# A two-layer diffusion trunk on one core: an output projection of eight full blocks, weight low parts by a fused operation, and mixing roots by ScalarE's ln and exp

## The chip, the core and the metric

The kernel runs on one core of a Trainium2 chip. The core has TensorE (PE; its weight loads stand in a row of their own, PEld), VectorE (DVE), ScalarE (ACT), GpSimd (POOL) and SyncE (SP), which here issues the DMAs. Each engine works through its own queue in order; semaphores tie them together. The metric is the device time of one execution in microseconds (us), the median of several runs.

## The reference, cut to what matters

A trunk of two layers works on 128 context tokens and 256 latent tokens together (T = 384). Each layer is a SwiGLU half, a token mixing, and a second SwiGLU half, each behind an RMSNorm with shift, scale and gate from a conditioning vector. The mixing projects the tokens once, runs three head groups (A: grouped attention; B: gated linear attention; C: differential attention) and projects their joined outputs back:

```
q, k of A and C:  x * rsqrt(mean(x*x) + EPS) * g          per head
out_a = softmax attention,              width 6 x 64 = 384
out_b = rms_norm(o_b, g_gla) * silu(b_r), width 4 x 64 = 256
out_c = rms_norm(out_c, g_c_out) * (1 - lam_init), width 4 x 96 = 384
out   = concatenate([out_a, out_b, out_c]) @ w_out        (1024 x 1024)
x     = x + gate * out
```

## The kernel before, in words

Activations lie transposed, 128 features on the partitions and 384 tokens along the row, in eight tiles `x[k]`. Each matmul with weights is done in three pieces (`mm3`): weights and activations are split into a high part that TensorE takes in its fp32r form and a low part that holds the rest, and high x high, high x low and low x high are summed in PSUM. `load_split` loads a weight tile (`wraw`, five buffers), ScalarE rounds the high part (`whi`, three buffers), VectorE subtracts to get the low part (`wlo`, three buffers). In the feed-forward halves VectorE also sums products for the modulation vectors (L254), and GpSimd subtracts the low parts of activations (`alo`, L477).

A mixing (`mixing`) is cut into named stages, and `ORDER` gives the order in which each layer's stages are written. `br`, `bq`, `bk`, `bv`, `wa`, `wv`, `wq` and `wk` are projections, `lg`, `de`, `st`, `L0` to `L6` and `go` belong to group B, `c0` to `c3` are the four heads of group C, `n0` and `n1` their norms (two heads each), `s0` and `s1` the splits into high and low parts, `p0` to `p2` and `o0` to `o2` the attention of group A. Tile, the layer that issues the program, keeps the data dependences and orders each engine's instructions by its own plan, so stages overlap. `lg` asks for ScalarE's table set with natural log and exp.

The inverse roots come from `newton`, all on VectorE: a first value by integer arithmetic on the bits, then three steps of three operations, 13 operations in all on 12 or 24 columns. A mixing has seven: one in `make_rstd`, one in `qk_norm` for each of `wa`, `wq`, `wk`, and one in `rsq_bcast` for `n0`, `n1` and `go` (which spreads the root over a row by transposes).

The projection reads nine blocks of 128 rows in the order of `KORD`: three of A, two of B, and four of C, one per head, of 96 rows, with the weights' last 32 rows of such a block at zero and not used. For each of eight output tiles it takes two loads, of five and four blocks:

```
for k0, k1 in ((0, 5), (5, 9)):
    w = load_split(I["wo"][l, m][:, k0 * P:k1 * P], (k1 - k0) * P)
    for k in range(k0, k1):
        n, hi, lo = mo[k]
        mm3(ps, w[0][:n, c:c + P], w[1][:n, c:c + P], hi, lo, k == 0, k == 8)
end_tile(l, 1, m, ps, acc, nxt, None)
```

Of the kernel before, what the change touches and what calls it, by code (L numbers as in the profile page):

```python
# [27 lines left out]
EPS = 1e-6  # L28
# [18 lines left out]
TW = T + 2  # L47
# [7 lines left out]
NPT = 3  # L55
# [5 lines left out]
NRM = (0, 1)  # L61
HV = (1, 1, 1, 1, 1, 1, 1, 1)
ORDER = (
    ("ha br bq hb bk wq bv lg rq de wk st L0 rk L1 cx wa wv L2 c0 L3 c1 L4 c2 ra L5 L6 n0 s0 c3 n1 p0 ax "
     "s1 go o0 p1 p2 o1 o2").split(),
    ("br ha hb bq bk bv lg L0 wq rq wk de L1 st rk L2 wa cx wv L3 c0 ra L4 c1 c2 L5 c3 n0 L6 p0 ax "
     "go o0 p1 s0 p2 o1 n1 s1 o2").split(),
)
KORD = (
    ("c0 c1 c2 c3 b0 b1 a0 a1 a2").split(),  # L70
    ("a0 b0 b1 c0 c1 a1 c2 c3 a2").split(),
)


# [7 lines left out]
def _build(ctx, tc, nc, I, O):  # L82
# [213 lines left out]

    def load_split(src, cols=WCOL):
        raw = wp.tile([P, WCOL], F32, tag="wraw", bufs=NRAW, name="wraw")
        di = nc.sync.dma_start(out=raw[:, :cols] if len(src.shape) == 2 else
                               raw[:, :cols].rearrange("p (j c) -> p j c", j=src.shape[1]), in_=src)  # L300
        hi = wp.tile([P, WCOL], F32R, tag="whi", bufs=3, name="whi")
        lo = wp.tile([P, WCOL], F32R, tag="wlo", bufs=3, name="wlo")
        S.activation(out=hi[:, :cols], in_=raw[:, :cols], func=AF.Copy)  # L303
        vi = V.tensor_tensor(out=lo[:, :cols], in0=raw[:, :cols], in1=hi[:, :cols].bitcast(F32), op=ALU.subtract)  # L304
        return hi, lo, vi, di

    def mm3(ps, lh, ll, rh, rl, start, stop):
# [4 lines left out]
    def newton(pool, ss, n, scale, parts, tag):  # L312

        m = pool.tile([P, n], F32, tag=tag + "m", name="nm")[:parts]
        V.tensor_scalar(out=m, in0=ss, scalar1=scale, scalar2=EPS, op0=ALU.mult, op1=ALU.add)
        s = pool.tile([P, n], I32, tag=tag + "s", name="ns")[:parts]
        V.tensor_scalar(out=s, in0=m.bitcast(I32), scalar1=1, scalar2=None, op0=ALU.logical_shift_right)
        y = pool.tile([P, n], F32, tag=tag + "y", bufs=2, name="ny")[:parts]
        V.tensor_scalar(out=y.bitcast(I32), in0=s, scalar1=-1.0, scalar2=float(0x5f3759df), op0=ALU.mult, op1=ALU.add)
        mh = pool.tile([P, n], F32, tag=tag + "h", name="nh")[:parts]  # L320
        V.tensor_scalar(out=mh, in0=m, scalar1=-0.5, scalar2=None, op0=ALU.mult)
        for _ in range(3):
            a = pool.tile([P, n], F32, tag=tag + "a", name="na")[:parts]
            V.tensor_tensor(out=a, in0=y, in1=y, op=ALU.mult)
            V.tensor_tensor(out=a, in0=a, in1=mh, op=ALU.mult)
            y2 = pool.tile([P, n], F32, tag=tag + "y", bufs=2, name="ny")[:parts]
            V.scalar_tensor_tensor(out=y2, in0=a, scalar=1.5, in1=y, op0=ALU.add, op1=ALU.mult)
            y = y2
        return y

    def rsq_bcast(pool, srcs, cols, scale, parts, tag, t, r):
# [5 lines left out]
        y = newton(pool, t.rearrange("p n (a b) -> p (n a) b", b=32)[:, :, 0], n * nb, scale, parts, tag)  # L337
# [223 lines left out]
    def mixing(l, us, acc, nxt):  # L561
        turn["own"] = {"mm": ("both",), "ax": ("ada",)}
        r_ = make_rstd(acc)
        with tc.tile_pool(name=f"mix{l}", bufs=1) as mp:
            def mt(shape, tag, bufs=1, dt=F32):
                return mp.tile(shape, dt, tag=tag, bufs=bufs, name=tag)
# [9 lines left out]
            s0 = mt([P, 2, 64], "s0")  # L576
# [79 lines left out]
            def qk_norm(pss, parts, n, d):  # L656

                w = n * d
                ss = mt([P, 3, 8], "ss", 2)
                xs = []  # L660
                for t, ps in enumerate(pss):
                    xg = t512()
                    for c, hn, gd, g in parts:
                        V.tensor_tensor(out=xg[:, c:c + hn * gd].rearrange("p (h d) -> p h d", h=hn),
                                        in0=ps[:, c:c + hn * gd].rearrange("p (h d) -> p h d", h=hn),
                                        in1=g[:, None, :].to_broadcast([P, hn, gd]), op=ALU.mult)
                    sq = t512(w)
# [3 lines left out]
                y = newton(mp, ss.rearrange("p a b -> p (a b)"), 24, 1.0 / d, P, "q")  # L671
# [78 lines left out]
            def a_out(i, pts):  # L750
                po = (mmps if PMM[6 + i] else axps)()[:, :T]
                for k in range(4):
                    for g in range(2):
                        r = slice(64 * g, 64 * g + 64)
                        if k == 0:
                            PE.matmul(po[r, 0:P], lhsT=av[:, 0, r], rhs=ptx[:, g, i, :], start=True, stop=True)
                        else:
                            PE.matmul(po[r, P:T], lhsT=av[:, k, r], rhs=pts[g][:, k - 1, :],  # L758
                                      start=(k == 1), stop=(k == 3))
                hi = hp.tile([P, TW], F32R, tag="h", name="ohi")[:, :T]  # L760
                S.activation(out=hi, in_=po, func=AF.Copy)
# [48 lines left out]
            cp = {}  # L810

            def c_first(j):
                cp[j] = mt([P, 2, T], "oc", 2)[:96], mt([P, 2, T], "pt", NPT)[:96], []
                c_next(j, 0)

            def c_next(j, i):
                oc, osq, pss = cp[j]
                c_head(2 * j + i, oc[:, i, :], osq[:, i, :], pss)

            def c_norm(j):  # L820
                oc, osq, pss = cp[j]
                r = rsq_bcast(mp, pss, T, 1.0 / 96, 96, "c", osq, osq)
                V.scalar_tensor_tensor(out=oc, in0=oc, scalar=gco[:96], in1=r, op0=ALU.mult, op1=ALU.mult)

            def c_split(j):
                oc = cp[j][0]
                for i in range(2):
                    hi = hp.tile([P, TW], F32R, tag="h", name="chi")[:96, :T]
                    S.activation(out=hi, in_=oc[:, i, :], func=AF.Copy)
                    lo = hp.tile([P, TW], F32R, tag="h", name="clo")[:96, :T]  # L830
                    V.tensor_tensor(out=lo, in0=oc[:, i, :], in1=hi.bitcast(F32), op=ALU.subtract)
                    moc.append((96, hi, lo))
# [112 lines left out]
            def gla_out():  # L945
# [31 lines left out]
                for i in range(2):  # L977
                    hi = hp.tile([P, TW], F32R, tag="h", name="bhi")[:, :T]
                    lo = hp.tile([P, TW], F32R, tag="h", name="blo")[:, :T]
                    S.activation(out=hi, in_=ot[:, i, :], func=AF.Copy)  # L980
                    V.tensor_tensor(out=lo, in0=ot[:, i, :], in1=hi.bitcast(F32), op=ALU.subtract)
                    mob.append((P, hi, lo))

            sv = {}

# [81 lines left out]


            turn["own"] = {"mm": ("both",), "ax": ()}
            mo = [{"a": moa, "b": mob, "c": moc}[n[0]][int(n[1])] for n in KORD[l]]  # L1070
            acc = new_acc()
            us = []
            for m in range(KT):
                ps = mmps()[:, :T]
                for k0, k1 in ((0, 5), (5, 9)):
                    w = load_split(I["wo"][l, m][:, k0 * P:k1 * P], (k1 - k0) * P)
                    for k in range(k0, k1):
                        c = (k - k0) * P
                        n, hi, lo = mo[k]
                        mm3(ps, w[0][:n, c:c + P], w[1][:n, c:c + P], hi, lo, k == 0, k == 8)  # L1080
# [138 lines left out]
```

## Time and profile before

| | |
|---|---|
| median of three timed runs | 1589.09 us (1588.32 to 1589.89) |
| the profiled execution's own time | 1599.75 us |
| its span, first to last instruction | 1597.9 us |
| PE busy | 1563.3 us, 9370 matmuls |
| DVE busy | 1229.3 us, 2294 instructions |
| ACT busy | 738.8 us, 1444 instructions |
| POOL busy | 196.2 us, 239 instructions |
| mean granted TensorE clock | 0.980 |

Busy times are sums over stages that differ; matmul ends are modelled, so a busy PE is not yet PE at its peak. The first layer's mixing lies at about 314 to 533 us of the span, the second's at about 1096 to 1315 us; all else is feed-forward. The granted clock is a share of 2.4 GHz; it is 1.0 or, at 1.2 GHz, 0.5.

### The profile page before, as it was taken

The numbers are of one execution on the slowest core, as the hardware profiler recorded it, in microseconds if no ns is written. First come the engines' busy times: TensorE is split into PE (matmuls) and PEld (weight loads), VectorE is DVE, ScalarE is ACT, GpSimd is POOL, SyncE is SP. The second block draws the span as 40 slices with busy tenths as digits, with TensorE's granted clock in tenths as the row PEclk, the third lists the DMA queues.
The fourth block names the chain that finished last, engine by engine and source line by source line (L and its number), as shares of the span: only waits on it lengthen the run. The fifth ranks groups of instructions, "written<-read, shape, count | busy, mean of one in ns | idle before, by whom it ended". The sixth has DMA issues, their size and how long they took to land.

```text
span 1597.9 us, 25055 instructions
## 1 busy us (share of the span) xinstructions
PE 1563.3 (98%) x9370; PEld 1464.0 (92%) x9370; DVE 1229.3 (77%) x2294; ACT 738.8 (46%) x1444; POOL 196.2 (12%) x239
## 2 busy tenths in 40 slices
PE   7999999999999999999999999999999999999999
PEld 5999999997558999999999999999875699999999
DVE  4799999888766888898968889667787767666532
ACT  4544433365466544443344444335546754444321
POOL 1211130030000211111001111102000011111100
PEclk9999999999789999999999999999898999999999
DMA  9677778542104566666666666543321064443441
GB/s 330 231 229 229 226 225 261 165 122 83 45 1 140 168 197 202 201 192 207 204 213 197 210 197 195 174 144 96 113 77 39 1 230 144 143 137 130 120 143 57
DMA packets 83230, 256.38 MB, mean 160 GB/s; under 512 B 10978, under 2 KB 19746, under 8 KB 82722
## 3 DMA queue, kind: packets, MB, share of 16 engines
q1 hardware_dynamic: 83108, 254.78, 50.3%
q8 instruction: 74, 1.21, 0.3%
q14 instruction: 48, 0.39, 0.1%
HBM read 251.99 MB, written 2.75 MB: 159 GB/s over the span
## 4 chain that ended last, share of the span: by engine, by line
PE 90%; DVE 6%; ACT 2%; issue 1%; DMA 1%; POOL 1%; SPq 0%; DVEq 0%; ACTq 0%; POOLq 0%
PE mm L308 20%; PE mm L310 20%; PE mm L309 20%; PE both L308 7%; PE both L309 7%; PE both L310 7%; PE mm L789 1%; DVE wlo L304 1%; PE ax L803 1%; PE ax L901 1%; PE ax L721 1%; DVE junk L254 1%; PE ax L807 0%; DVE ht L397 0%; PE ax L758 0%
## 5 line engine op out<-in xcount | busy, mean ns | idle before, releaser
L303 ACT ACTIVATE whi<-wraw 128x1024 fp32r<-128x1024 f32 (+4 forms) x358 | 348.4, 975 | 461.2 <-PE mm L309 259.1
L304 DVE TENSOR_TENSOR wlo<-wraw,whi 128x1024 fp32r<-128x1024 f32 (+4 forms) x358 | 451.8, 1264 | 131.0 <-ACT whi L303 129.0
L310 PE MATMUL mm<-h,wlo 128*128 128x386 f32 x1096 | 373.3, 341 | 2.5 <-DVE wlo L304 2.5
L308 PE MATMUL mm<-h,whi 128*128 128x386 f32 x1096 | 372.8, 341 | 2.6 <-POOL h L367 1.4
L309 PE MATMUL mm<-h,whi 128*128 128x386 f32 x1096 | 372.5, 340 | 0.0
L254 DVE SCALAR_TENSOR_TENSOR junk<-araw,cb 128x1024 f32<-128x1024 f32 x256 | 312.3, 1220 | 0.8
L310 PEld LDWEIGHTS mm<-h,wlo 128*128 128x128 f32 x1096 | 208.0, 190 | 4.2 <-DVE wlo L304 3.5
L308 PEld LDWEIGHTS mm<-h,whi 128*128 128x128 f32 x1096 | 207.6, 190 | 4.6 <-ACT whi L303 1.7
L309 PEld LDWEIGHTS mm<-h,whi 128*128 128x128 f32 x1096 | 207.6, 189 | 1.6 <-issue 0.7
L477 POOL TENSOR_TENSOR alo<-s,ahi 128x384 fp32r<-128x384 f32 x88 | 115.5, 1314 | 641.5 <-ACT ahi L475 614.9
L309 PE MATMUL mm<-alo,whi 128*128 128x384 f32 x528 | 177.9, 337 | 0.0
L310 PE MATMUL mm<-ahi,wlo 128*128 128x384 f32 x528 | 177.9, 337 | 0.0
L308 PE MATMUL mm<-ahi,whi 128*128 128x384 f32 x528 | 177.9, 337 | 0.0
L308 PE MATMUL both<-h,whi 128*128 128x386 f32 x360 | 122.5, 340 | 0.0
L309 PE MATMUL both<-h,whi 128*128 128x386 f32 x360 | 122.1, 339 | 0.0
L310 PE MATMUL both<-h,wlo 128*128 128x386 f32 x360 | 122.0, 339 | 0.0
L475 ACT ACTIVATE ahi<-s 128x384 fp32r<-128x384 f32 x88 | 46.3, 526 | 129.4 <-DVE s L472 129.3
L309 PEld LDWEIGHTS mm<-alo,whi 128*128 128x128 f32 x528 | 99.2, 188 | 0.0
L310 PEld LDWEIGHTS mm<-ahi,wlo 128*128 128x128 f32 x528 | 99.2, 188 | 0.0
L308 PEld LDWEIGHTS mm<-ahi,whi 128*128 128x128 f32 x528 | 99.2, 188 | 0.0
L469 DVE TENSOR_TENSOR u<-mm,rstd 128x384 f32<-128x384 f32 x66 | 36.6, 554 | 60.8 <-PE mm L310 60.8
L467 ACT ACTIVATE s<-s,bc 128x128 f32<-128x128 f32 (+1 forms) x176 | 70.7, 449 | 8.0 <-ACT bc L418 0.7
(365 smaller groups left out, 2446.7 us busy)
## 6 DMA issues: line engine op xcount, KB each, us to landing
wraw<-in_wgu SPq DMA_DIRECT2D x170, 512.0 KB, 4.2
araw<-in_w_adat SPq DMA_DIRECT2D x128, 512.0 KB, 4.0
wraw<-in_wd SPq DMA_DIRECT2D x64, 512.0 KB, 4.2
wraw<-in_wd SPq DMA_DIRECT2D x32, 384.0 KB, 3.5
araw<-in_w SPq DMA_DIRECT2D x16, 512.0 KB, 5.6
wraw<-in_wo SPq DMA_DIRECT2D x16, 320.0 KB, 3.0
wraw<-in_wit SPq DMA_DIRECT2D x8, 512.0 KB, 3.4
wraw<-in_wa SPq DMA_DIRECT2D x8, 512.0 KB, 3.6
```

What stands on the lines that cost most here:

```text
L254: V.scalar_tensor_tensor(out=junk, in0=w, scalar=1.0, in1=self.cb[:, c, :], op0=ALU.mult, op1=ALU.mult, accum_out=self.acc[:, f, c:c + 1])
L303: S.activation(out=hi[:, :cols], in_=raw[:, :cols], func=AF.Copy)
L304: vi = V.tensor_tensor(out=lo[:, :cols], in0=raw[:, :cols], in1=hi[:, :cols].bitcast(F32), op=ALU.subtract)
L308: PE.matmul(ps, lhsT=lh, rhs=rh, start=start, stop=False)
L309: PE.matmul(ps, lhsT=lh, rhs=rl, start=False, stop=False)
L310: return PE.matmul(ps, lhsT=ll, rhs=rh, start=False, stop=stop)
L467: S.activation(out=s[:, a:b], in_=s[:, a:b], func=AF.Silu, bias=bg[:, c:c + 1])
L469: vi = V.tensor_tensor(out=u, in0=pu[:, :T], in1=r, op=ALU.mult)
L475: S.activation(out=hi, in_=s, func=AF.Copy)
L477: G.tensor_tensor(out=lo, in0=s, in1=hi.bitcast(F32), op=ALU.subtract)
L721: pi = PE.transpose(ps[:, i * P:(i + 1) * P], p[:, i, :], ident)
L789: PE.matmul(pp[m], lhsT=qtc[r, h, (t + 1) * P:(t + 2) * P], rhs=ktc[r, h, 0:T], start=True, stop=True)
```

## The change

The four C heads are packed into three blocks of 128 rows: heads 0 to 2 keep their 96 rows, and head 3's 96 rows go as three strips of 32 into rows 96 to 127 of these blocks. `c_norm(1)` writes the strips. `wo_parts` cuts the weight load that holds the C blocks accordingly, since the weights' layout in memory stays. The projection then has eight blocks, in two loads of four, and the stage orders move: the C splits follow both norms.

`load_split` gets its low part by a fused multiply and subtract. `newton` saves the integer shift, by a multiplication by -0.5. The six roots of a mixing that are not `make_rstd`'s go to `rsq_act`: ln and exp on ScalarE and one Newton step on VectorE.

```diff
 ORDER = (
-    ("... c2 ra L5 L6 n0 s0 c3 n1 p0 ax "
-     "s1 go o0 p1 p2 o1 o2").split(),
+    ("... c2 ra L5 L6 n0 c3 n1 p0 ax "
+     "s0 s1 go o0 p1 p2 o1 o2").split(),
     ("... c1 c2 L5 c3 n0 L6 p0 ax "
-     "go o0 p1 s0 p2 o1 n1 s1 o2").split(),
+     "go n1 o0 p1 s0 p2 s1 o1 o2").split(),
 KORD = (
-    ("c0 c1 c2 c3 b0 b1 a0 a1 a2").split(),
-    ("a0 b0 b1 c0 c1 a1 c2 c3 a2").split(),
+    ("c0 c1 c2 b0 b1 a0 a1 a2 c3").split(),
+    ("a0 b0 b1 a1 c0 c1 c2 a2 c3").split(),
...
     def load_split(src, cols=WCOL):
+        for rows, cs, part in (src if isinstance(src, list) else [(slice(0, P), slice(0, cols), src)]):
+            dst = raw[rows, cs]
...
+            di = nc.sync.dma_start(out=dst, in_=part)
-        vi = V.tensor_tensor(out=lo[:, :cols], in0=raw[:, :cols], in1=hi[:, :cols].bitcast(F32), op=ALU.subtract)
+        vi = V.scalar_tensor_tensor(out=lo[:, :cols], in0=raw[:, :cols], scalar=1.0, in1=hi[:, :cols].bitcast(F32),
+                                    op0=ALU.mult, op1=ALU.subtract)
...
+    def rsq_act(pool, ss, n, scale, parts, tag):
+        mh = pool.tile([P, n], F32, tag=tag + "h", name="nh")[:parts]
+        V.tensor_scalar(out=mh, in0=ss, scalar1=-0.5 * scale, scalar2=-0.5 * EPS, op0=ALU.mult, op1=ALU.add)
+        y = pool.tile([P, n], F32, tag=tag + "y", bufs=2, name="ny")[:parts]
+        S.activation(out=y, in_=mh, func=AF.Ln, scale=-2.0)
+        S.activation(out=y, in_=y, func=AF.Exp, scale=-0.5)
+        a = pool.tile([P, n], F32, tag=tag + "a", name="na")[:parts]
+        V.tensor_tensor(out=a, in0=y, in1=y, op=ALU.mult)
+        V.tensor_tensor(out=a, in0=a, in1=mh, op=ALU.mult)
+        y2 = pool.tile([P, n], F32, tag=tag + "y", bufs=2, name="ny")[:parts]
+        V.scalar_tensor_tensor(out=y2, in0=a, scalar=1.5, in1=y, op0=ALU.add, op1=ALU.mult)
+        return y2
...
             def c_norm(j):
                 oc, osq, pss = cp[j]
                 r = rsq_bcast(mp, pss, T, 1.0 / 96, 96, "c", osq, osq)
-                V.scalar_tensor_tensor(out=oc, in0=oc, scalar=gco[:96], in1=r, op0=ALU.mult, op1=ALU.mult)
+                n = 2 - j
+                V.scalar_tensor_tensor(out=oc[:96, :n], in0=oc[:96, :n], scalar=gco[:96], in1=r[:, :n],
+                                       op0=ALU.mult, op1=ALU.mult)
+                if j:
+                    for i in range(3):
+                        q = slice(32 * i, 32 * i + 32)
+                        V.scalar_tensor_tensor(out=cp[i // 2][0][96:P, i % 2, :], in0=oc[q, 1, :], scalar=gco[q],
+                                               in1=r[q, 1, :], op0=ALU.mult, op1=ALU.mult)
...
+            def wo_parts(w, k0, k1):
+                if not k0 <= kc < k1:
+                    return w[:, k0 * P:k1 * P]
+                b = (kc - k0) * P
+                parts = [(slice(0, 96), slice(0, (k1 - k0) * P), w[0:96, k0 * P:k1 * P]),
+                         (slice(96, P), slice(b, b + 3 * P),
+                          w[0:96, KT * P:(KT + 1) * P].rearrange("(j p) c -> p j c", j=3))]
+                for k in range(k0, k1):
+                    if not kc <= k < kc + 3:
+                        parts.append((slice(96, P), slice((k - k0) * P, (k - k0 + 1) * P), w[96:P, k * P:(k + 1) * P]))
+                return parts
...
-                for k0, k1 in ((0, 5), (5, 9)):
-                    w = load_split(I["wo"][l, m][:, k0 * P:k1 * P], (k1 - k0) * P)
+                for k0, k1 in ((0, 4), (4, 8)):
+                    w = load_split(wo_parts(I["wo"][l, m], k0, k1), (k1 - k0) * P)
```

## Rows read from the trace of the kernel before

**Rows 1.** Busy time by stretch: us, then each engine's busy us, clock, DMA

```profile
core 0: us, PE busy (x) PEld busy (x) DVE busy (x) ACT busy (x) POOL busy (x), PEclk, DMA share, GB/s
...
354.00:416.00 62.00, 60.27 (x456) 49.36 (x457) 55.20 (x130) 34.86 (x75) 7.61 (x8) 0.97 0.28 83
...
536.00:817.00 281.00, 281.00 (x1590) 280.90 (x1589) 242.56 (x388) 116.90 (x209) 33.77 (x39) 1.00 0.61 192
```

**Rows 2.** The same view, around each layer's output projection

```profile
487.90:499.92 12.02, 12.02 (x79) 9.00 (x77) 7.23 (x15) 8.62 (x21) 0.00 (x0) 1.00 0.10 27
499.92:532.72 32.80, 32.80 (x188) 32.74 (x188) 19.75 (x37) 18.52 (x28) 3.65 (x10) 1.00 0.75 249
1270.94:1280.69 9.75, 9.75 (x62) 8.07 (x62) 3.53 (x8) 6.58 (x16) 0.00 (x0) 0.82 0.12 35
1280.69:1314.99 34.30, 34.30 (x197) 34.29 (x196) 20.65 (x39) 18.66 (x28) 3.69 (x10) 1.00 0.71 237
```

**Rows 3.** The same two early stretches, L308's matmuls and weight loads alone

```profile
487.90:499.92 12.02, 3.32 (x11) 1.88 (x11) 1.00 0.10 27
...
1270.94:1280.69 9.75, 2.74 (x7) 1.67 (x7) 0.82 0.12 35
```

**Rows 4.** Groups by line and shape: busy us, mean ns of one, idle before

```profile
L310 PE MATMUL mm<-chi,wlo 96*128 96x384 f32 x48 | 16.4, 341 | 0.0
...
L310 PE MATMUL mm<-ohi,wlo 128*128 128x384 f32 x36 | 12.3, 341 | 0.0
```

**Rows 5.** The chain of waits, layer 0: start us, us, what

```profile
472.47 0.19 DVE nm L315
```

**Rows 6.** The chain of waits, layer 1

```profile
1248.97 0.28 DVE nm L315
...
1252.23 0.18 DVE na L325
...
1261.52 0.19 DVE nm L315
...
1264.11 0.98 DVE e L338
```

**Rows 7.** DMA issues by line: count, size, median us from issue to landing

```profile
wraw<-in_wo SPq DMA_DIRECT2D x16, 320.0 KB, 3.0
```

**Rows 8.** Groups by line and shape, VectorE

```profile
L831 DVE TENSOR_TENSOR clo<-oc,chi 96x384 fp32r<-96x384 f32 x8 | 4.3, 550 | 0.8 <-ACT chi L829 0.6
...
L823 DVE SCALAR_TENSOR_TENSOR oc<-oc,sp,pt 96x768 f32<-96x768 f32 x4 | 4.0, 1011 | 0.0
```

**Rows 9.** ScalarE: one group by line and shape, then four timeline rows

```profile
L862 ACT ACTIVATE dec<-c 128x1 f32<-128x1 f32 x2 | 0.4, 187 | 0.0
...
347.44 0.84 ACT L303 ACTIVATE whi<-wraw 128x768 fp32r<-128x768 f32 x1 [1.71 <-PE both L310]
...
353.74 1.28 ACT L631 ACT_TABLE_LOAD   x1
355.03 0.58 ACT L638 ACTIVATE e<-ax,sp 128x384 f32<-128x384 f32 x1
...
1259.28 0.58 ACT L697 ACTIVATE p<-mm,mx 128x384 f32<-128x384 f32 x1
```

**Rows 10.** Timeline of GpSimd and VectorE where both work on tiles in SBUF

```profile
84.51 1.92 POOL L477 TENSOR_TENSOR alo<-s,ahi 128x384 fp32r<-128x384 f32 x1 [7.07 <-ACT ahi L475]
...
85.75 1.76 DVE L254 SCALAR_TENSOR_TENSOR junk<-araw,cb 128x1024 f32<-128x1024 f32 x1
...
563.49 2.02 DVE L304 TENSOR_TENSOR wlo<-wraw,whi 128x1024 fp32r<-128x1024 f32 x1
...
565.91 1.21 DVE L304 TENSOR_TENSOR wlo<-wraw,whi 128x1024 fp32r<-128x1024 f32 x1
```

**Rows 11.** Busy time by stretch, at the two longest falls of the clock

```profile
417.70:420.65 2.95, 0.49 (x5) 0.00 (x1) 2.95 (x8) 0.73 (x3) 0.00 (x0) 1.00 0.48 148
421.50:448.80 27.30, 26.83 (x112) 13.60 (x110) 15.07 (x46) 14.27 (x37) 0.00 (x0) 0.50 0.00 1
...
1213.40:1227.00 13.60, 13.60 (x42) 6.66 (x42) 7.26 (x23) 8.01 (x21) 0.00 (x0) 0.50 0.00 0
```

More of the change, by code (lines that the diff above doesn't have):

```diff
@@ L63 @@
 ORDER = (
-    ("ha br bq hb bk wq bv lg rq de wk st L0 rk L1 cx wa wv L2 c0 L3 c1 L4 c2 ra L5 L6 n0 s0 c3 n1 p0 ax "
-     "s1 go o0 p1 p2 o1 o2").split(),
+    ("ha br bq hb bk wq bv lg rq de wk st L0 rk L1 cx wa wv L2 c0 L3 c1 L4 c2 ra L5 L6 n0 c3 n1 p0 ax "
+     "s0 s1 go o0 p1 p2 o1 o2").split(),
     ("br ha hb bq bk bv lg L0 wq rq wk de L1 st rk L2 wa cx wv L3 c0 ra L4 c1 c2 L5 c3 n0 L6 p0 ax "
-     "go o0 p1 s0 p2 o1 n1 s1 o2").split(),
+     "go n1 o0 p1 s0 p2 s1 o1 o2").split(),
 )
 KORD = (
-    ("c0 c1 c2 c3 b0 b1 a0 a1 a2").split(),
-    ("a0 b0 b1 c0 c1 a1 c2 c3 a2").split(),
+    ("c0 c1 c2 b0 b1 a0 a1 a2 c3").split(),
+    ("a0 b0 b1 a1 c0 c1 c2 a2 c3").split(),
 )
@@ L298, in load_split @@
         raw = wp.tile([P, WCOL], F32, tag="wraw", bufs=NRAW, name="wraw")
-        di = nc.sync.dma_start(out=raw[:, :cols] if len(src.shape) == 2 else
-                               raw[:, :cols].rearrange("p (j c) -> p j c", j=src.shape[1]), in_=src)
+        for rows, cs, part in (src if isinstance(src, list) else [(slice(0, P), slice(0, cols), src)]):
+            dst = raw[rows, cs]
+            if len(part.shape) == 3:
+                dst = dst.rearrange("p (j c) -> p j c", j=part.shape[1])
+            di = nc.sync.dma_start(out=dst, in_=part)
         hi = wp.tile([P, WCOL], F32R, tag="whi", bufs=3, name="whi")
@@ L315, in newton @@
         V.tensor_scalar(out=m, in0=ss, scalar1=scale, scalar2=EPS, op0=ALU.mult, op1=ALU.add)
-        s = pool.tile([P, n], I32, tag=tag + "s", name="ns")[:parts]
-        V.tensor_scalar(out=s, in0=m.bitcast(I32), scalar1=1, scalar2=None, op0=ALU.logical_shift_right)
         y = pool.tile([P, n], F32, tag=tag + "y", bufs=2, name="ny")[:parts]
-        V.tensor_scalar(out=y.bitcast(I32), in0=s, scalar1=-1.0, scalar2=float(0x5f3759df), op0=ALU.mult, op1=ALU.add)
+        V.tensor_scalar(out=y.bitcast(I32), in0=m.bitcast(I32), scalar1=-0.5, scalar2=float(0x5f3759df),
+                        op0=ALU.mult, op1=ALU.add)
         mh = pool.tile([P, n], F32, tag=tag + "h", name="nh")[:parts]
@@ L336, in rsq_bcast @@
             V.transpose(out=t[:, i, :], in_=s)
-        y = newton(pool, t.rearrange("p n (a b) -> p (n a) b", b=32)[:, :, 0], n * nb, scale, parts, tag)
+        y = rsq_act(pool, t.rearrange("p n (a b) -> p (n a) b", b=32)[:, :, 0], n * nb, scale, parts, tag)
         V.transpose(out=r.rearrange("p n (a b) -> p (n a) b", b=32),
@@ L670, in qk_norm @@
                     xs.append(xg[:, :w].rearrange("p (h d) -> p h d", h=n))
-                y = newton(mp, ss.rearrange("p a b -> p (a b)"), 24, 1.0 / d, P, "q")
+                y = rsq_act(mp, ss.rearrange("p a b -> p (a b)"), 24, 1.0 / d, P, "q")
                 return xs, [y[:, 8 * t:8 * t + 8][:, :, None].to_broadcast([P, n, d]) for t in range(3)]
@@ L763, in a_out @@
                 V.tensor_tensor(out=lo, in0=po, in1=hi.bitcast(F32), op=ALU.subtract)
-                moa.append((P, hi, lo))
+                moa.append((hi, lo))
             ptc_ = []
@@ L812, in c_first @@
             def c_first(j):
-                cp[j] = mt([P, 2, T], "oc", 2)[:96], mt([P, 2, T], "pt", NPT)[:96], []
+                cp[j] = mt([P, 2, T], "oc", 2), mt([P, 2, T], "pt", NPT)[:96], []
                 c_next(j, 0)
@@ L817, in c_next @@
                 oc, osq, pss = cp[j]
-                c_head(2 * j + i, oc[:, i, :], osq[:, i, :], pss)
+                c_head(2 * j + i, oc[:96, i, :], osq[:, i, :], pss)
             def c_norm(j):
@@ L822, in c_norm @@
                 r = rsq_bcast(mp, pss, T, 1.0 / 96, 96, "c", osq, osq)
-                V.scalar_tensor_tensor(out=oc, in0=oc, scalar=gco[:96], in1=r, op0=ALU.mult, op1=ALU.mult)
-            def c_split(j):
[L826 to L832, printed above, removed]
+                n = 2 - j
[6 more added lines that the diff above has]
+                                               in1=r[q, 1, :], op0=ALU.mult, op1=ALU.mult)
+            def c_split(j):
+                for i in range(2 - j):
+                    oc = cp[j][0][:, i, :]
+                    hi = hp.tile([P, TW], F32R, tag="h", name="chi")[:, :T]
+                    S.activation(out=hi, in_=oc, func=AF.Copy)
+                    lo = hp.tile([P, TW], F32R, tag="h", name="clo")[:, :T]
+                    V.tensor_tensor(out=lo, in0=oc, in1=hi.bitcast(F32), op=ALU.subtract)
+                    moc.append((hi, lo))
             bv = mt([P, 3, 256], "bv")
@@ L981, in gla_out @@
                     V.tensor_tensor(out=lo, in0=ot[:, i, :], in1=hi.bitcast(F32), op=ALU.subtract)
-                    mob.append((P, hi, lo))
+                    mob.append((hi, lo))
             sv = {}
@@ L1069, in mixing @@
             turn["own"] = {"mm": ("both",), "ax": ()}
-            mo = [{"a": moa, "b": mob, "c": moc}[n[0]][int(n[1])] for n in KORD[l]]
+            mo = [{"a": moa, "b": mob, "c": moc}[n[0]][int(n[1])] for n in KORD[l][:KT]]
+            kc = KORD[l].index("c0")
+            def wo_parts(w, k0, k1):
[9 more added lines that the diff above has]
+                return parts
             acc = new_acc()
@@ L1074, in mixing @@
                 ps = mmps()[:, :T]
-                for k0, k1 in ((0, 5), (5, 9)):
-                    w = load_split(I["wo"][l, m][:, k0 * P:k1 * P], (k1 - k0) * P)
+                for k0, k1 in ((0, 4), (4, 8)):
+                    w = load_split(wo_parts(I["wo"][l, m], k0, k1), (k1 - k0) * P)
                     for k in range(k0, k1):
                         c = (k - k0) * P
-                        n, hi, lo = mo[k]
-                        mm3(ps, w[0][:n, c:c + P], w[1][:n, c:c + P], hi, lo, k == 0, k == 8)
+                        hi, lo = mo[k]
+                        mm3(ps, w[0][:, c:c + P], w[1][:, c:c + P], hi, lo, k == 0, k == KT - 1)
                 end_tile(l, 1, m, ps, acc, nxt, None)
```

## The prediction

> **What bounds the kernel now.** I read the table by stretches first. In a feed-forward half (536 to 817 us) TensorE is busy for the whole 281 us while VectorE works 242.56 and ScalarE 116.90 [rows 1]: there TensorE alone counts, and what the other engines save is worth nothing. In the first part of a mixing (354 to 416 us) VectorE is busy 55.20 of 62 us and TensorE 60.27, so both are near their limit [rows 1]. The end of a mixing I split by the source line of `mm3` [rows 2, 3]. From 499.92 to 532.72 us, and from 1280.69 to 1314.99, nothing but the output projection runs on TensorE: 188 matmuls in 32.80 us and 197 in 34.30, 0.1745 and 0.174 us from one to the next, with no gap. Before that lies a stretch in which projection matmuls of the first blocks slip in among the attention's; TensorE shows as busy all through it (12.02 of 12.02 and 9.75 of 9.75), but only 11 and 7 of L308's 144 projection matmuls stand there [rows 3], a third of what `mm3` issues. Last comes the chain of waits. In most of the kernel it runs over TensorE; in the mixings' ends it leaves it, and there Newton roots lie on it, small VectorE operation after small operation [rows 5, 6].
>
> **Output projection.** Eight blocks for nine: 8 output tiles x 3 matmuls x 2 layers = 48 matmuls fewer. The blocks dropped were filled to 96 rows, and a 96-row matmul costs what a 128-row one costs (341 ns each [rows 4]), so filling the other three blocks to 128 rows is free: 48 x 0.1745 = -8.4 us. If the matmuls that slip in early only filled holes, the part that counts is smaller: 18 of 144 stand there, so -8.4 x 126/144 = -7.3. TensorE shows busy in those stretches, though by modelled ends, so I take -8.0.
>
> The weights of a tile come in two loads of 512 columns instead of 640 and 512. The load that holds the c blocks is now cut into three transfers (96 rows, three 32-row strips, the remaining 32-row piece), 4 transfers per tile instead of 2, 32 more in all. A load lands 3.0 us after its issue [rows 7]; five raw buffers at one load in 12 matmuls (2.1 us) give about 10 us of lead. Cost 0, if the cover holds; were it gone, each of 16 cut loads could hold TensorE for part of 3.0 us, and that is a rival below. SP's queue issues more, and it also issues the next half's modulation weights, which have slack.
>
> **The c tail.** `c_norm(1)` loses half its 768-wide product and gains three 32-row strips; `c_split` does three splits instead of four. The 768-wide product took 1.01 us and a 384-wide VectorE subtraction 0.55 [rows 8], so on VectorE 1.01 becomes 4 x about 0.55 = 2.2 (+1.2), and -0.55 for the split. In layer 0 the chain passes through just this place, and block c0 now has to wait for the last head. Bounds 0 and +1.2 per layer; I take +0.9 over both, because in layer 0 the first projection matmuls come 15 us after `c_norm(1)`'s root begins (487.90 against 472.47 [rows 3, 5]) and most of the delay is slack. In layer 1 the block order a0 b0 b1 a1 puts late a1 in the first load: fewer matmuls are ready early, which is inside the -7.3 above.
>
> **Roots.** Twelve Newton roots (six per mixing) shrink from 13 VectorE operations to 4, plus Ln and Exp on ScalarE. A root that ran nearly undisturbed took from 1261.52 to 1264.11, 2.59 us, at 0.18 us per operation [rows 6]. The new one: 4 x 0.18 on VectorE; two small ScalarE operations at 0.19 (the nearest is an Exp on 128x1, 187 ns [rows 9]); two handovers, nearly nothing in the same trace. That is 1.1 to 1.3 us if ScalarE is free, a gain of 1.3. But ScalarE's queue is in order too, and in the attention it is full of softmax rows of 0.58 us [rows 9]; I charge one of them per root, which leaves 0.7. Three roots lie openly on the chain: `c_norm(1)` of layer 0 (from 472.47 us on), the same of layer 1 (1248.97 to its last operation at 1252.23) and `gla_out` of layer 1 [rows 5, 6]. 3 x 0.7 = -2.1 us, with -3.9 (ScalarE free) and +1 (more than two rows ahead) as bounds.
>
> The other nine free VectorE of 9 x 9 x 0.18 = 14.6 us. In the first part of a mixing it was 89% busy [rows 1], so some of it comes through, the more so as ropes and scores queue behind; elsewhere others cover it. Bounds 0 and -5; I take -1.2, near the lower, as TensorE is just as full there. The six kept roots lose one operation each; three are on or near the path: -0.3 at most, -0.2.
>
> **Tables.** In layer 0 stage `wq` comes ahead of `lg`, which fetches the table with Ln and Exp; its root therefore runs while the Silu table is in, and asks for one or two more loads. A load takes 1.28 us and the next activation follows at once (353.74 + 1.28, then 355.03 [rows 9]): 1.3 to 2.6 us of ScalarE, which idled 1.71 us ahead of a weight split there, waiting for TensorE to free a buffer [rows 9]. That idle time covers it, and behind it the two other buffers; were both gone, TensorE would wait the whole. I take +0.3 of 0 to +2.6. The Trainium skill (ScalarE: Activation LUTs, What ACT_TABLE_LOAD costs) adds a drain and puts each switch at about 2.66 us; by it two switches would be 5.3 us and the sum some us higher. The trace shows no such drain behind the load, so I go by the row.
>
> **Weight low parts.** The fused form replaces a plain subtraction on every weight tile. Undisturbed, the plain one took 1.21 us for 1024 columns; behind GpSimd's running `alo` it took 2.02 [rows 10]. One could hope that the fused form escapes this. It doesn't: L254, the same fused form at the same width, started at 85.75 inside a GpSimd operation that ran from 84.51 to 86.43 and took 1.76 [rows 10]. So 0; and in the feed-forward halves a gain or a loss of 0.1 us per tile would be hidden by TensorE anyway.
>
> **Sum.** -8.0 + 0.9 - 2.1 - 1.2 - 0.2 + 0.3 = -10.3 us. The profiled execution ran 1599.75 us, of which 1597.9 is the span; it would become 1589.4. It is 10.7 us above the median of the timed runs, 1589.09; the same sum there gives 1578.8.
>
> **Rivals.**
> *TensorE alone counts (27%).* The roots give nothing back, because others queue in their place: -8.0 + 0.9 + 0.3 = -6.8, 1582.3 us. For it: in 487 to 500 us TensorE shows busy throughout.
>
> *The clock (18%).* From 421.50 to 448.80 us TensorE's granted clock was 0.50, the 1.2 GHz level, and TensorE was busy 26.83 of 27.30 us while VectorE had 15.07; ahead of it TensorE had stood for most of 2.95 us, waiting for a VectorE that worked without pause [rows 11]. The root of `wa` just ahead loses 9 x 0.18 = 1.6 us of VectorE. Layer 1's fall lasted 13.60 us [rows 11]. If layer 0's becomes like it, half of 13.7 us is given back: -6.8 more, 1572 us. Against it: layer 1's shows that the fall can come anyhow; and a new order of the instructions may as well lengthen one, 1585 us.
>
> *ScalarE's queue holds VectorE (6%): slower.* Both queues are in order: VectorE's next operation of the root waits for Exp, Exp for what is queued ahead of it, and behind it in VectorE's queue stand row maxima and the splits that feed TensorE. With four softmax rows ahead (4 x 0.58 = 2.3 us, against the 1.3 gained) a root costs 1.0 more than now: 12 x 1.0 against -6.8 gives +5.2, 1594.3 us. It decides from 0.6 us per root upward. Against it: the earliest three roots of a mixing fall outside the softmax, and a root has other VectorE work that can be put between.
>
> *The cut loads set the pace (1%): slower.* If three transfers land one after another, 9 us for 12 matmuls of 2.1 us, the projection stretches by 6.9 us on each of 16 loads, +110 us, 1689. The Trainium skill (DMA: Bandwidth & Descriptors, in its table of rules) says that transfers to disjoint partition ranges share the same engines and serialise. Against it: the stretch moved 249 GB/s with loads lying in each other's time [rows 2].
>
> **How the numbers follow.** 45% for the forecast (its own range 1575 to 1581 us), 27, 18, 6 and 1% as above, 3% for several small losses that end near no change. About 0.2% (3.2 us) is what a measurement of this kernel can tell from no change, so 1585.9 is the line to faster. Of the clock's 18% I count 2 as a fall that grows and eats the gain. Faster: 45 + 27 + 16 = 88%; same: 2 + 3 = 5%; slower: 6 + 1 = 7%. The range reaches down to the clock's 1572 with the free-ScalarE end of the roots (-1.8) and some more of VectorE's relief (-2), 1568; and up to the first rival's 1582.3 with the tables' upper end (+2.3) and the projection's lower one (+0.7) and a us for the c tail, 1586.
>
> **What would show it.** The projection's own stretches: 192 matmuls per mixing instead of 216, still 0.174 us apart, 9322 matmuls in all. Twelve Ln and twelve Exp of about 0.2 us, VectorE with some 110 operations fewer, and the three roots on the chain at 1.3 to 2 us. ACT_TABLE_LOAD 8 or 9 times instead of 7. `wlo` still 2.0 us behind `alo`. Wrong would be: gaps of TensorE ahead of a projection tile, idle time of VectorE ended by Exp of more than 1 us, or a granted clock of 0.50 over clearly more or less than the 27.3 and 13.6 us of before.

## The result and the profile after

The changed kernel takes 1576.33 us (median of 7 executions, 1575.56 to 1585.42) beside 1589.44 of before (7 executions): ratio 0.9902, 95% interval 0.9877 to 0.9928. The forecast was 1578.8 with a range of 1568 to 1586, faster at 88%. The profiled execution ran 1575.88 us, its span 1574.1.

The forecast's number held; its reasons held only in part, and that shows as soon as the two profiles are laid side by side. The spans differ by 23.8 us, the medians by 13. The page of the changed kernel opens with its span and each engine's busy time:

```profile
span 1574.1 us, 24928 instructions
...
PE 1538.8 (98%) x9322; PEld 1446.5 (92%) x9322; DVE 1216.2 (77%) x2184; ACT 740.7 (47%) x1468; POOL 195.6 (12%) x239
```

There are 9322 matmuls, 48 fewer, as forecast. The windows around each layer's output projection (us, busy us and count of each engine, granted clock, DMA share, GB/s), to compare with [rows 2]:

```profile
491.37:520.60 29.23, 29.23 (x169) 29.23 (x169) 19.15 (x38) 18.06 (x29) 3.24 (x8) 1.00 0.80 256
1258.70:1289.70 31.00, 30.89 (x176) 30.44 (x176) 20.40 (x40) 18.97 (x31) 3.27 (x8) 1.00 0.80 259
```

29.23 us for 169 matmuls is 0.173 us from one to the next, 31.00 for 176 is 0.176: the pace of [rows 2], over fewer matmuls. From issue to landing the pieces of a cut load take 2.5 to 2.8 us (medians: 192 KB 2.6, 48 KB 2.8, 16 KB 2.5), against 3.0 for a whole one before [rows 7].

A root, in the timeline of VectorE and ScalarE:

```profile
476.39 0.18 DVE L337 TENSOR_SCALAR nh<-e 128x24 f32<-128x24 f32 x1
476.61 0.22 ACT L339 ACTIVATE ny<-nh 128x24 f32<-128x24 f32 x1 [0.20 <-DVE nh L337]
...
477.25 0.20 ACT L340 ACTIVATE ny<-ny 128x24 f32<-128x24 f32 x1
477.48 0.18 DVE L342 TENSOR_TENSOR na<-ny 128x24 f32<-128x24 f32 x1 [0.91 <-ACT ny L340]
477.70 0.18 DVE L343 TENSOR_TENSOR na<-na,nh 128x24 f32<-128x24 f32 x1
477.92 0.18 DVE L345 SCALAR_TENSOR_TENSOR ny<-na,ny 128x24 f32<-128x24 f32 x1
```

It takes 1.71 us against 2.59 [rows 6]; between Ln and Exp ScalarE did something else. In layer 1 (1160 to 1262 us) no root stands on the chain of waits any more; further back this profile's chain does not reach.

Then the clock. Windows at the two falls of the attention in layer 0, each with the stretch ahead of it:

```profile
426.60:430.00 3.40, 2.81 (x10) 1.11 (x9) 3.06 (x9) 3.22 (x9) 0.00 (x0) 0.99 0.02 5
430.00:433.40 3.40, 3.40 (x19) 2.01 (x18) 1.48 (x5) 2.12 (x8) 0.00 (x0) 0.50 0.00 0
464.10:467.50 3.40, 1.77 (x16) 0.81 (x16) 3.10 (x9) 2.89 (x15) 0.00 (x0) 1.00 0.01 2
467.50:474.30 6.80, 6.71 (x19) 2.84 (x20) 3.07 (x8) 5.54 (x15) 0.00 (x0) 0.50 0.01 2
```

0.50, the 1.2 GHz level, stands here over 3.4 and 6.8 us, where before had 27.3 [rows 11]; in the whole execution before stood at 0.50 for 64.9 us and the changed kernel for 17.1, and for its last 0.7. Ahead of both falls TensorE had stood for a part of the time (2.81 of 3.40 us busy, 1.77 of 3.40).

The last difference is in a place the change did not mean to touch: down-projection matmuls, TensorE alone, in a window of 80 us inside each of the four feed-forward halves. First before, then the changed kernel:

```profile
220.00:300.00 80.00, 80.00 (x463) 1.00 0.74 234
722.00:802.00 80.00, 80.00 (x455) 1.00 0.65 204
1002.00:1082.00 80.00, 80.00 (x463) 1.00 0.52 155
1504.00:1584.00 80.00, 80.00 (x463) 1.00 0.39 117
```

```profile
223.00:303.00 80.00, 80.00 (x455) 1.00 0.74 232
710.00:790.00 80.00, 80.00 (x455) 1.00 0.64 202
990.00:1070.00 80.00, 80.00 (x455) 1.00 0.49 151
1479.00:1559.00 80.00, 80.00 (x455) 1.00 0.39 117
```

At a clock of 1.00 and with no gap, 463 matmuls fit into 80 us in three halves of before, 455 in one; the changed kernel has 455 in all four. From the starts of single matmuls, that is 173.3 or 176.7 ns from one to the next, on average over a half's 528.

### The profile page after: what moved, and what is told of

The parts are those of the page before. It is cut to its first block, busy times and chain, and to the rows that moved or that the text cites. A ratio compares the mean times of both kernels' runs of the same rounds, so it can differ in the third digit from the quotient of the medians.

```text
span 1574.1 us, 24928 instructions
## 1 busy us (share of the span) xinstructions
PE 1538.8 (98%) x9322; PEld 1446.5 (92%) x9322; DVE 1216.2 (77%) x2184; ACT 740.7 (47%) x1468; POOL 195.6 (12%) x239
## 5 line engine op out<-in xcount | busy, mean ns | idle before, releaser
L306 ACT ACTIVATE whi<-wraw 128x1024 fp32r<-128x1024 f32 (+3 forms) x358 | 346.7, 970 | 451.5 <-PE mm L313 259.0
L307 DVE SCALAR_TENSOR_TENSOR wlo<-wraw,whi 128x1024 fp32r<-128x1024 f32 (+3 forms) x358 | 450.7, 1262 | 127.8 <-ACT whi L306 125.6
```

What stands on the lines that cost most here:

```text
L307: vi = V.scalar_tensor_tensor(out=lo[:, :cols], in0=raw[:, :cols], scalar=1.0, in1=hi[:, :cols].bitcast(F32), op0=ALU.mult, op1=ALU.subtract)
```

## Experiments

**How they are read.** Every execution comes with its span S and mean granted clock c; 2 x (1 - c) x S is then its time at the low level (0.50). Over 89 executions of the kernel before, 28 to 70 us of it and 1585 to 1602 us of time, the time is 1573.3 + 0.42 x low-level time, and 0.9 us of scatter is left. So each difference splits into clock (0.42 x the difference in low-level time) and the rest, "at equal clock". The table has both, against the executions of before of the same set of runs; n is the executions of the kernel and of before.

| kernel | n | median us | before | ratio, 95% | low level, us | before | at equal clock |
|---|---|---|---|---|---|---|---|
| e1 before again | 12, 29 | 1593.1 | 1593.7 | 0.9997 (0.9972 to 1.0022) | 49 | 49 | -0.5 ±0.3 |
| e2 projection alone | 12, 29 | 1587.8 | 1593.7 | 0.9952 (0.9929 to 0.9975) | 52 | 49 | -8.7 ±0.4 |
| e3 roots alone | 6, 29 | 1581.2 | 1593.7 | 0.9922 (0.9893 to 0.9952) | 27 | 49 | -3.3 ±0.2 |
| e4 fused form alone | 12, 29 | 1591.1 | 1593.7 | 0.9986 (0.9962 to 1.0010) | 44 | 49 | -0.1 ±0.2 |
| e5 changed kernel again | 6, 17 | 1581.5 | 1595.5 | 0.9918 (0.9886 to 0.9950) | 31 | 52 | -5.2 ±0.5 |
| e6 table fetched early | 6, 17 | 1578.1 | 1595.5 | 0.9903 (0.9871 to 0.9935) | 28 | 52 | -5.8 ±0.7 |
| e7 two roots (wa) | 12, 17 | 1595.0 | 1595.5 | 0.9995 (0.9969 to 1.0020) | 50 | 52 | -0.1 ±0.3 |
| e8 VectorE held up | 6, 17 | 1634.7 | 1595.5 | 1.0262 (1.0230 to 1.0294) | 84 | 52 | +28.2 ±0.4 |
| e9 64 bytes more | 6, 14 | 1573.4 | 1590.0 | 0.9897 (0.9865 to 0.9928) | 31 | 44 | -10.7 ±0.4 |
| e10 32 bytes more | 9, 14 | 1581.3 | 1590.0 | 0.9924 (0.9897 to 0.9951) | 34 | 44 | -8.0 ±0.4 |
| e11 96 bytes more | 6, 14 | 1570.3 | 1590.0 | 0.9882 (0.9849 to 0.9915) | 23 | 44 | -10.5 ±0.8 |
| e12 shorter first guess | 12, 17 | 1592.5 | 1593.3 | 0.9981 (0.9956 to 1.0006) | 38 | 51 | +2.5 ±0.4 |

(± is one standard error of the difference. It leaves out the error of the method: e1, in which nothing was changed, gives -0.5; and the factor is 0.42 too over the 100 executions of the other kernels, each kernel with a constant of its own, but 0.34 to 0.51 in single kernels, which for a difference of 20 us in low-level time is another 1 to 2 us.) Medians of before wander between 1589.4 and 1595.5 from one set of runs to the next, with its low-level time; that is why the last column is needed.

**e1: before, unchanged.**

> The kernel of before, unchanged, for the clock and span of each of its executions. The profiled execution of before had TensorE at the 1.2 GHz level for 64.9 us (mean granted clock 0.980) and a span of 1597.9 us, that of after 17.1 us (0.994) and 1574.1 us. Theory (the sum of the prediction: fewer matmuls, shorter roots): the executions of before near 1589 us have a mean clock near after's, 0.990 or more, and the 13 us between the medians are the change's own work. Rival (the clock): before stands at 0.985 or lower in most executions, near 50 us or more at the low level, after rarely, and then at an equal clock the two kernels lie clearly less than 10 us apart. The ratio is 1.000 under both.

Executions near 1589 us have a clock of 0.988, those near 1600 one of 0.980 to 0.982: neither theory is right alone. Before does stand at 49 us of low level on average, so the clock is a large part of the difference. The profile of e1 has no fall of 27 us in layer 0, where the first profile of before had one [rows 11], but one of 10.2 and one of 13.7: where a single profile has its falls is chance.

**e2: the projection alone.** The changed kernel with three edits put back:

```diff
-        vi = V.scalar_tensor_tensor(out=lo[:, :cols], in0=raw[:, :cols], scalar=1.0, in1=hi[:, :cols].bitcast(F32),
-                                    op0=ALU.mult, op1=ALU.subtract)
+        vi = V.tensor_tensor(out=lo[:, :cols], in0=raw[:, :cols], in1=hi[:, :cols].bitcast(F32), op=ALU.subtract)
...
-                y = rsq_act(mp, ss.rearrange("p a b -> p (a b)"), 24, 1.0 / d, P, "q")
+                y = newton(mp, ss.rearrange("p a b -> p (a b)"), 24, 1.0 / d, P, "q")
```

(so too in `rsq_bcast`; the third is the first guess of `newton`, in two operations again).

> Only the output projection over 8 full blocks (with its order of stages, cut weight loads and c tail); all Newton roots and the plain subtraction stay as before. Sum of the prediction: -8.0 + 0.9 = -7.1 us, 1582.3 us beside 1589.4; TensorE-alone rival: nearly the whole gain of the change, -8 us or more, stands here and the roots give nothing. Clock rival: less than 40 us at the low level in most executions only if the order of the stages decides it; with the Newton roots left in, this theory expects the fall behind the root of wa in layer 0 (27.3 us at 0.50 in before) to come back.

-8.7 at equal clock, where the sum had -7.1 and the matmuls alone -8.4: the c tail costs nothing that can be seen. The low-level time stays, 52 us, and the profile has 27.3 us at 0.50 behind the first c heads again.

**e3: the roots alone.** Before with `rsq_act`, called in `rsq_bcast` and `qk_norm`.

> Only the twelve roots by Ln and Exp; projection over nine blocks, order and weight split as before. Sum of the prediction: -2.1 - 1.2 + 0.3 = -3.0 us, 1586.4 us. TensorE-alone rival: 0, 1589.4. ScalarE-queue rival: slower by up to 12 us. Clock rival: the fall of the clock behind wa in layer 0 shrinks from 27.3 us towards 13.6 or less, and the time falls by 5 to 10 us, more than the sum gives.

Two effects at once: -3.3 at equal clock, close to the sum's -3.0 and not the 0 of the rival in which TensorE alone counts, and -9.0 through the clock (27 us of low level instead of 49). So the clock's gain comes with the roots, not with the projection.

**e4: the fused form alone.** `scalar_tensor_tensor` in `load_split`, nothing else.

> Only the fused form of the weights' low parts (scalar_tensor_tensor for tensor_tensor on every weight tile). Prediction: no change, within 1.5 us of 1589.4, the mean of wlo at 1262 ns beside 1264 before. A rival that the fused form runs free of GpSimd would show wlo below 1.22 us in the feed-forward halves and up to 3 us less in the mixings. If the time moves by more than 3 us with wlo unchanged, it is the clock's falls that have moved, and the clock of each execution has to show it.

No change. The rows of the 1024-wide tiles, busy us and mean ns of one, are alike, before and then the changed kernel:

```profile
L304 DVE TENSOR_TENSOR wlo<-wraw,whi 128x1024 fp32r<-128x1024 f32 x258 | 367.4, 1425 | 105.0 <-ACT whi L303 103.7 <-DMA wraw<-in_wgu 1.1
L307 DVE SCALAR_TENSOR_TENSOR wlo<-wraw,whi 128x1024 fp32r<-128x1024 f32 x258 | 367.7, 1427 | 108.5 <-ACT whi L306 107.9
```

In e4 it is 1425 ns too. In each of the three profiles 67 of the 258 take 2.01 to 2.02 us, every one while GpSimd works on a tile, and the others 1.22: the fused form waits as the plain one does. (The 1262 ns over all shapes, against 1264 before, come from the projection's narrower tiles; e4 has 1264.)

**e5: the changed kernel again.**

> The changed kernel once more, unchanged, beside the same executions of before as the other runs. Theory (less work, and a clock that falls for less time): before stood at the low clock level for about 49 us of an execution on average (41 executions of the first call), the changed kernel for about 25 (7 executions); again 20 to 30 us, a median of 1574 to 1578, and, with half of the low-level time taken off, 8 to 11 us less than before: 8 from the projection, 1 to 3 from the roots. The feed-forward stretch without any fall, 561.4 us in the first profile of after and 559.6 in every profile of before, should be 559.6 here, if that 0.3% belongs to the chip. Rival (the roots give nothing but clock, and the clock of 7 executions was luck): mean low-level time near 45 us, median 1583 to 1586.

The low-level time is 31 us, near what was expected; the median, 1581.5, is above the 1574 to 1578. And at equal clock the gain is 5.2, not 8 to 11, while e2 and e3 add up to 12.0; and the stretch without falls is 561.4 us on the chip that gave before 559.6. The 0.3% belongs to the kernel, and the halves above show where: 455 instead of 463 matmuls.

**e6: the table fetched once, ahead of `wq`.**

```diff
             def c_proj(w):
+                if l == 0 and w == 0:
+                    tc.keep_in_program_order(S.preload_act_table_set("natural_log_exp_and_others"))
```

(and in `decays` only in layer 1).

> The changed kernel, with the table that holds Ln and Exp fetched once ahead of the first root of layer 0, in place of the two loads for that root and the third in the decays' stage: 7 table loads instead of 9. Theory: the idle time of TensorE of 1.14 us at 356.71 us, which neither profile of before has, comes from the two loads and goes away: 1 to 2.5 us faster than the changed kernel at the same clock. Rival (the loads were covered, the sum's lower bound): same time within 1 us at the same clock, idle time of TensorE unchanged.

In the changed kernel the root of `wq` meets both loads, and TensorE stands behind it (timelines of ScalarE and TensorE):

```profile
349.90 1.28 ACT L339 ACT_TABLE_LOAD   x1
351.20 0.22 ACT L339 ACTIVATE ny<-nh 128x24 f32<-128x24 f32 x1
351.44 1.28 ACT L340 ACT_TABLE_LOAD   x1
352.73 0.22 ACT L340 ACTIVATE ny<-ny 128x24 f32<-128x24 f32 x1
```

```profile
357.85 0.41 PE L1060 MATMUL ada<-cst,t 128*128 128x128 f32 x2 [1.14 <-DVE t L1052]
```

With the early fetch this idle time is gone, but the time is only 0.6 us lower at equal clock, with an error of 0.9: not told apart from nothing. A cost above 2 us, such as the upper end of the tables' term, is unlikely by this; the +0.3 stands. The Trainium skill (ScalarE: Activation LUTs, What ACT_TABLE_LOAD costs) adds a drain to each load, 2.66 us for a switch. The rows above show no drain: they have the activation 0.01 to 0.02 us behind each load, and the second load 0.02 us behind the activation ahead of it.

**e7: only the two roots of `wa`.**

```diff
-                y = newton(mp, ss.rearrange("p a b -> p (a b)"), 24, 1.0 / d, P, "q")
+                y = (rsq_act if d == 64 else newton)(mp, ss.rearrange("p a b -> p (a b)"), 24, 1.0 / d, P, "q")
```

> Before, with only the root of wa in each layer by Ln and Exp (2 of the 12). Theory (the clock in layer 0 falls because TensorE waits for a VectorE that is late by this root): most of what the twelve roots gave comes back with these two: TensorE's wait ahead of the second c head's scores shrinks from 2.46 us to below 1.6, low-level time from 49 to 25 to 38 us on average, time 4 to 10 us below before. Rival (the twelve roots act by their sum, each a little): low-level time 42 us or more, time at most 2 us below before.

This theory fell. TensorE's wait ahead of the second c head did shrink, from 2.46 to 1.82 us, but the low-level time stayed at 50 us, and the time at before's. The clock's gain is not to be had from this one root.

**e8: TensorE made to stand in the feed-forward halves.** `hold` is 8, 13 and 18 for one weight tile in each of three halves:

```diff
+        for _ in range(hold):
+            V.tensor_tensor(out=raw, in0=raw, in1=raw, op=ALU.max)
         hi = wp.tile([P, WCOL], F32R, tag="whi", bufs=3, name="whi")
```

> Before, with VectorE held up at one weight tile in each of three feed-forward halves, in which no profile shows a fall of the clock: 8, 13 and 18 operations of 1.2 us on the raw weights (each the maximum of the tile with itself) ahead of the split of one tile, so that TensorE runs out of split weights. Theory (the granted clock falls behind a stretch in which TensorE stood still): where TensorE's gaps add up to 1.5 us or more, a stretch at the low level follows within 10 us, of 3.4 to 27 us in length, and the half is longer by the gap and half of that stretch; where the gap stays below 0.5 us, no fall. Rival (the falls belong to the mixings, to their small matmuls or to what VectorE and ScalarE do there): gaps of several us without a fall; each half longer by its gaps alone.

TensorE's gaps are 3.99, 16.48 and 15.12 us, and each brings a fall. Timeline of TensorE, then a window from shortly ahead of the first gap's end:

```profile
638.57 0.69 PE L311 MATMUL mm<-h,whi 128*128 128x386 f32 x1 [3.99 <-ACT bc L421]
```

```profile
637.50:647.70 10.20, 8.63 (x24) 7.17 (x25) 9.85 (x14) 3.38 (x5) 1.88 (x1) 0.50 0.44 147
```

0.50 for 10.2 us, most of it after TensorE worked again. At the two long gaps it is 17.1 us each, begun while TensorE still stood. In these halves before's profile has 1.00 throughout (one of them in [rows 1]). The pair of halves between the mixings is 27.9 us longer: 21.0 of gaps and half of the 12.6 us that TensorE worked at the low level, 6.3, give 27.3. The last half: 15.1 + 2.9 = 18.0 of 18.2. So a stand of 4 us or more was enough to bring a fall in a feed-forward half, all three times; VectorE worked nearly all through these stands, so its part is not told apart.

For the mixings' falls this is not the whole cause. A short stand does not always bring one: of 1.88 us, ending at 1117.0 us, it had a fall within 1 us in the first profile of before, and the same stand in e1 had none. And a fall can come with hardly a stand ahead of it: in the first profile of before at 1128.1 us, behind 6.8 us in which TensorE shows no gap at all, and in e1 at 457.7 us. Windows of e1:

```profile
423.60:427.00 3.40, 1.95 (x7) 0.91 (x7) 3.35 (x12) 2.55 (x9) 0.00 (x0) 1.00 0.26 77
427.00:437.20 10.20, 10.20 (x22) 4.96 (x22) 7.01 (x22) 6.27 (x16) 0.00 (x0) 0.50 0.01 2
437.20:457.70 20.50, 20.29 (x257) 12.89 (x255) 17.35 (x59) 14.67 (x38) 0.50 (x1) 1.00 0.01 2
457.70:471.40 13.70, 13.70 (x49) 8.05 (x47) 3.56 (x12) 5.58 (x15) 1.77 (x3) 0.50 0.00 1
```

Ahead of the second fall TensorE shows busy for 20.29 of 20.50 us, by modelled ends, with the attention's small matmuls. So the rival, that the falls belong to the mixings and their small matmuls, is refuted as the only cause, but may be one of two.

**e9, e10, e11: the tiles' addresses.** In the changed kernel, with 16, 8 or 24 elements:

```diff
-        mh = pool.tile([P, n], F32, tag=tag + "h", name="nh")[:parts]
+        mh = pool.tile([P, n + 16 * (tag == "n")], F32, tag=tag + "h", name="nh")[:parts, :n]
```

> The changed kernel with 64 bytes added to one small tile of the root's helper, so that the tiles of the feed-forward activations (ahi, alo) stand at the addresses of before again; the order of instructions on every engine is that of the changed kernel. Theory (addresses): the change's shorter first guess dropped a small tile, by which all of these tiles moved by 64 bytes, and each of the 2111 matmuls that read them became 2.5 ns longer (176.65 against 174.12 ns from one to the next): these matmuls return to 174.1 ns, the feed-forward pair between the mixings from 561.4 to 559.6 us, and the time falls by 5.3 us at the same clock. Rival (the 2.5 ns come from the other work that runs beside these matmuls, the fused form for the weights above all): no change, 561.4 us.

> The same with 32 bytes: the tiles then begin on a multiple of 64 bytes, which they do neither before nor after. Theory (addresses, a start off a multiple of 64 costs): these 2111 matmuls at 174.1 ns or less, 5 us or more below the changed kernel at the same clock. Rival (only the start within 128 or 512 bytes counts, by another rule): any value from 174 to 177, and then e11 tells which.

> The same with 96 bytes: again on a multiple of 64, but the other one of 128. If a multiple of 64 is what counts, the same times as with 32 bytes; if the place within 128 bytes counts, 32 and 96 bytes differ, and the four starts together (352, 384, 416 and 448 bytes within 512) show which is fastest.

The order of instructions is the same in all of them. With 64 bytes, the same windows:

```profile
223.00:303.00 80.00, 80.00 (x463) 1.00 0.74 233
715.50:795.50 80.00, 80.00 (x464) 1.00 0.66 208
994.50:1074.50 80.00, 80.00 (x455) 1.00 0.50 151
1488.50:1568.50 80.00, 80.00 (x463) 1.00 0.39 117
```

With 96 bytes:

```profile
222.00:302.00 80.00, 80.00 (x454) 1.00 0.72 232
707.00:787.00 80.00, 80.00 (x464) 1.00 0.66 209
986.00:1066.00 80.00, 80.00 (x464) 1.00 0.52 156
1473.00:1553.00 80.00, 80.00 (x463) 1.00 0.39 117
```

Three halves are fast again in both; 3 x 528 x 3.33 ns = 5.3 us, and by the table the two are 5.5 and 5.3 us faster than e5 at equal clock. With 32 bytes the halves stand between (456 to 458 matmuls in 80 us) and 2.8 us come back. The cause is shown: 64 bytes of address. The rule behind it is not: a start on a multiple of 64 bytes gave the middle pace in e10 and the fast one in e11, e9 has the addresses of before and yet another half slow, and the same addresses give both paces within one kernel. At the addresses of before, which half stays slow goes with the projection: the second in all six profiles with the nine-block one, the third in the two with the eight-block one (e2 and e9).

**e12: the shorter first guess alone.**

```diff
-        s = pool.tile([P, n], I32, tag=tag + "s", name="ns")[:parts]
-        V.tensor_scalar(out=s, in0=m.bitcast(I32), scalar1=1, scalar2=None, op0=ALU.logical_shift_right)
...
-        V.tensor_scalar(out=y.bitcast(I32), in0=s, scalar1=-1.0, scalar2=float(0x5f3759df), op0=ALU.mult, op1=ALU.add)
+        V.tensor_scalar(out=y.bitcast(I32), in0=m.bitcast(I32), scalar1=-0.5, scalar2=float(0x5f3759df),
+                        op0=ALU.mult, op1=ALU.add)
```

> Before, with only the shorter first guess of the Newton roots (one VectorE operation on each of the 18 roots fewer, and one small tile fewer, by which the feed-forward tiles stand 64 bytes lower, as in the changed kernel). Prediction's own term, extended to all 18 roots: -0.3 to -1 us. Theory (addresses): the down-projection matmuls go at 176.7 ns in all four feed-forward halves, instead of in one of four as before, and that costs 3 x 528 x 3.3 ns = 5.3 us at the same clock, so 4 to 5 us slower than before at the same clock. Rival (it takes the projection's or the roots' other edits as well): halves at 173.3 ns as before, no loss.

All four halves are slow, without the projection or the new roots:

```profile
223.00:303.00 80.00, 80.00 (x455) 1.00 0.72 231
718.50:798.50 80.00, 80.00 (x455) 1.00 0.65 203
998.50:1078.50 80.00, 80.00 (x454) 1.00 0.49 152
1494.00:1574.00 80.00, 80.00 (x455) 1.00 0.39 117
```

At equal clock it is 2.5 us slower than before, less than the 4 to 5 expected: if the halves cost the 5.3, the operation saved on each of the 18 roots gives 2.8 back (the sum had 0.2, for the six kept ones). It also lowers the low-level time to 38 us, and so comes out level in the median.

## Why the number was right and the reasons only partly

The sum was -10.3 us. With the addresses put right (e9) the change is worth -10.7 ±0.4 at equal clock. As it stands it is worth -5.2, and some 9 us through the clock besides. The parts run alone (e2, e3, e4) add to -12.1, 1.4 us more than e9 gives; whether they overlap or the method errs by that much is open.

- **Output projection, -8.0, and c tail, +0.9:** together -8.7 ±0.4 (e2) for -7.1. This fits the matmuls' full 8.4 and a hidden tail, at its lower bound of 0; the two were not run apart. The cut loads cost nothing that shows: TensorE has no gap in layer 0's window above and 0.11 us in layer 1's. The Trainium skill (DMA: Bandwidth & Descriptors, Rules for kernel authors) says that two transfers to disjoint partition halves serialise, as they share the same engines. The trace agrees in that the pieces land in order, but 0.2 us apart (490.2, 490.4 and 490.6 us for the first load issued after 487 us); the rival's 9 us a load took the whole time from issue to landing three times, and nearly all of it overlaps.
- **Roots, -2.1 - 1.2, and tables, +0.3:** -3.3 ±0.2 (e3) for -3.0. Of the three roots that the sum priced, at 1.3 to 2 us, `c_norm(1)` takes 1.9 us in layer 0 but 3.4 in layer 1, and `gla_out` of layer 1 1.7. Of all twelve, nine take 1.6 to 2.5. Two in layer 1 take 3.4 and 3.5, because Ln comes 1.9 and 1.4 us behind its input on a full ScalarE, and the one that fetches its tables 4.3; that is the ScalarE-queue rival's mechanism, in two roots of twelve and too little to decide. Idle time of VectorE ended by Exp of more than 1 us, a named sign of being wrong, does occur twice (2.31 us at the table loads, 2.36 at `c_norm(1)` of layer 1), off the chain as far as it reaches.
- **Weight low parts, 0:** 0 (e4).
- **Kept roots, -0.2:** the step that failed. Counting one operation saved, I overlooked that its tile went with it and that every tile allocated behind it moved by 64 bytes. It lost 5.3 us in stretches where, by [rows 1], TensorE alone counts. The lesson was in before's trace, had I counted matmuls per half: its second half ran at 455 in 80 us beside 463 in the others.
- **The clock, taken as a rival with 18%:** it came true beside the forecast, not in place of it. I had named it as a sign of being wrong if 0.50 stood over clearly less than 27.3 and 13.6 us; it did, but so it did in e1, so one profile could not tell. The size, 9 us, is near the 6.8 that the rival gave; its cause was wrong. The root of `wa` alone changes nothing (e7), all twelve together bring low-level time from 49 to 27 us (e3, ±4), one operation less on each of eighteen brings it from 51 to 38 (e12, ±4). What is shown is that shorter roots everywhere make the falls fewer or shorter, and that a long stand of TensorE brings one (e8). That the roots work by taking stands away is argued, not shown; what decides a fall in the mixings, and why one and the same program spends 28 to 70 us at the low level, stays open.

So that the median landed 2.5 us from the forecast is luck: a loss of 5.3 and a gain of 9, both left out of the sum, partly cancelled.

The fastest version run is e11, the changed kernel with 96 bytes of filling: 1570.26 us, ratio 0.9882 (0.9849 to 0.9915). e9 equals it at equal clock; the 3 us between their medians is low-level time, 23 against 31 us.

## What to carry to other kernels

Before a difference of one per cent is explained, fit the time of many executions against their granted clock and compare at equal clock: a change can be worth as much through the time that TensorE spends at its low level (here 9 us) as through the work that it saves. Count matmuls per fixed window in a stretch that nothing else limits: a change of some bytes in one small tile can move every tile behind it and alter the pace of thousands of matmuls that the diff does not touch. An operation that is removed takes its tile along, and that belongs in the sum.

## What was not expected of the hardware

The same 128x384 matmul, back to back at a clock of 1.00, runs at 173.3 or 176.7 ns on average over a half, or, with 32 bytes of filling, at 175.6 to 176.0; which of these is the same in both profiles of before and in both of the changed kernel, and changes with the addresses of the tiles. A stand of 4 us brought TensorE's clock to 0.50 for 10.2 us. And for the first root ScalarE fetched a table ahead of Ln and another ahead of Exp, 1.28 us each, though the table fetched at 358.9 us for the decays then serves both in the five roots of layer 0 that follow.
